# Sums of input blocks taken from PSUM while rows are turned, turns tied behind named products, and four raw weight buffers in a ConvFFN kernel

## The chip, the cores and the metric

The kernel runs on one core of one Trainium2 chip. The metric is the device time of one execution in microseconds (us). The engines are TensorE (PE, matmuls; PEld are its weight loads), VectorE (DVE), ScalarE (ACT), GpSimd (POOL) and SyncE (SP, which here starts the weight transfers). Each engine works its own list in order and waits where an input or a buffer isn't ready.

## The reference

One layer of a decoder for 512 prompt rows, 16 meta rows and 8 × 8 sample rows, D = 1024, D_FF = 2816. The change lies between the token mixing and the end of the ConvFFN:

```python
    mix = jax.nn.sigmoid(gate_a) * (o_a @ p['w_branch_a']) + jax.nn.sigmoid(gate_b) * (o_b @ p['w_branch_b'])
    x = x + rmsnorm(mix @ p['w_out'], p['ln_mix_post'])

    xn = rmsnorm(x, p['ln_ffn_pre'])
    up, gate = jnp.split(xn @ p['w_ffn_in'], 2, axis=-1)
    gate, new_ffn_conv = causal_dwconv(gate, ffn_conv_buf, p['ffn_conv_w'], p['ffn_conv_b'])
    x = x + rmsnorm((jax.nn.gelu(gate) * up) @ p['w_down'], p['ln_ffn_post'])
```

All is float32. The product `mix @ w_out`, the product `xn @ w_ffn_in` and the convolution, Gelu and gating behind it are what the change rearranges.

## The kernel before

**Split products.** A float32 product is made of three matmuls over parts: each operand is divided into `hi` (ACT casts it, line 315) and `lo` (DVE takes the difference, line 316). Line 273 issues every matmul, line 421 every transpose. Tiles `whi`/`wlo` and `hw`/`lw` are weights, `owhi`/`owlo` the two halves of w_out, `fhi11` to `flo22` the turned rows (first digit: half of D, second: half of the columns), `gt` in the output projection the mixed rows.

**Output projection** (`out_proj`). Five row tiles i (0: 64 sample and 2 meta rows; 1 to 4: 128 prompt rows each) times two halves g of w_out: ten products (i, g), each 24 matmuls of 512 columns. After a tile's second product `finish` normalises, adds the residual, normalises again (y), has PE turn the rows (eight transposes to two PSUM banks) and splits them into `fhi`/`flo`. The scheduler places the transposes with a lowered priority.

**ConvFFN input** (`ffn_in`). w_ffn_in has 22 column blocks m of 128 for the gate and 22 for the value u. Blocks m = 0, 1, 2 are plain: four products per block (gate and u, column half 0 and 1) of 24 matmuls. `conv` then runs the gate through line 1804 (ACT), 1806 (two DVE steps) and Gelu (line 1809, ACT), and `times` (1819, 1820) multiplies by u straight from PSUM, which frees u's bank. `differences` makes r1 to r4, sums of blocks of the turned rows, line 1638, on DVE and POOL, and splits them to `fhit`/`flot`.

**The loop**, m = 3 to 21, is a seven-product scheme: p1, p7 of the block before, p5, p2, p6, p4 of the block before, p3, each 12 matmuls. Weights are combined from the four 512-row blocks a11, a12 (gate, tiles `wraw`) and a21, a22 (u, tiles `raw`): POOL makes s1 = a21 + a22 and s3 = a11 − a21, DVE makes s2 = s1 − a11 and s4 = a12 − s2 (tile `sw`, line 1718), and each is divided into `hw`/`lw`. a22 is divided as block "22". Line 1752 is ACT's copy of a product that others are added to, lines 1758 to 1764 add it to the gate (`add_g`), line 1829 adds p7 to u half 1, and then p4 accumulates on the same bank. Three buffers for `raw` and the order of the program decide when SP can start a transfer. Order within an engine is set by the scheduler from the program's order, priorities and buffers.

Of the kernel before, what the change touches and what calls it, by code (L numbers as in the profile page):

```python
# [20 lines left out]
NB = 8  # L21
# [129 lines left out]
class Body:  # L151
# [39 lines left out]
    def run(self):  # L191
# [14 lines left out]
        with ExitStack() as sm:  # L206
# [50 lines left out]
            for key in ("12", "22"):  # L257
                for e in self.f[key]:
                    nc.scalar.copy(e[:, :, 288:290], self.c("zero").unsqueeze(2).to_broadcast([128, 4, 2]))
            with ExitStack() as s:  # L260
                self.out_proj(self.pool(s, "wout"), wo0)
            swo.close()
            self.ftpool = self.pool(sm, "ft", side="right")
            self.ffn_in(sf, self.pool(sm, "gx", side="right"))
# [5 lines left out]
    def mm(self, out, lhsT, rhs, **kw):  # L270
        n = math.prod(rhs.shape[1:])
        self.work += (1.68e-3 if lhsT.dtype == F32 and lhsT.shape[1] > 32 else 0.42e-3) * n
        self.nc.tensor.matmul(out, lhsT, rhs, **kw)  # L273
# [970 lines left out]
    def meta_attention(self, pool):  # L1244
# [5 lines left out]
        mx = self.t(self.small, [128, 1], "mmx")  # L1250
# [36 lines left out]
    def prompt_rows(self, pool, h, st, on, order):  # L1287
# [3 lines left out]
        for i in order:  # L1291
            n = NM + 128 * (i + 1)
            pr = [self.t(pool, [128, 528], f"S{m}", bufs=2) for m in range(2)]
            mxs = [self.t(self.small, [128, 2], "mx", bufs=4) for m in range(2)]
# [14 lines left out]
            for s, mx in zip(pr, mxs):  # L1309
                nm = self.t(self.small, [128, 1], "nm", bufs=4)  # L1310
                nc.vector.tensor_scalar(nm, mx[:, 1:2], -1.0, None, op0=ALU.mult)
                sm = self.t(self.small, [128, 1], "sm", bufs=4)
                nc.scalar.activation(s[:, :n], s[:, :n], AF.Exp, bias=nm, accum_out=sm)
                rc = self.t(self.small, [128, 1], "rc", bufs=4)
# [27 lines left out]
    def head_norm(self, pool, on):  # L1342
        nc = self.nc
        rows, nh = on.shape[0], on.shape[1]
        ss = self.t(self.small, [128, 4], "hss", bufs=2)[:rows, :nh]
# [9 lines left out]
    def sample_attention(self, pool):  # L1355
# [33 lines left out]
        for pr in range(NB // 2):  # L1389
# [3 lines left out]
            mx = self.t(self.small, [128, 5], "smx", bufs=2)  # L1393
# [33 lines left out]
            m1 = self.t(self.small, [128, 1], "m1", bufs=2)  # L1427
# [52 lines left out]
    def soft(self, S, mx, kind):  # L1480
        nc = self.nc
        nm = self.t(self.small, [128, 1], "nm", bufs=4)
        nc.vector.tensor_scalar(nm, mx, -1.0, None, op0=ALU.mult)
        sm = self.t(self.small, [128, 1], "sm", bufs=4)
        nc.scalar.activation(S, S, AF.Exp, bias=nm, accum_out=sm)
        rs = self.t(self.small, [128, 1], "rc", bufs=4)
# [61 lines left out]
    def out_proj(self, pool, wo0):  # L1548
        nc, a = self.nc, self.a
# [8 lines left out]
        ys, sums = {}, {}  # L1558

        def product(i, g):  # L1560
# [3 lines left out]
            for k in range(8):  # L1564
                mh, ml = (e[:, c0 : c0 + n] for e in self.mixed[k])
                self.mm(p[:n], mh, whi[:, k], start=k == 0, stop=False)
                self.mm(p[:n], mh, wlo[:, k], start=False, stop=False)
                self.mm(p[:n], ml, whi[:, k], start=False, stop=k == 7)
            if g == 0:
                ys[i] = self.t(pool, [128, D], "y", bufs=4)  # L1570
# [5 lines left out]
        def finish(i):  # L1576
# [12 lines left out]
            xs = ys.pop(i)  # L1589
# [8 lines left out]
            with self.tc.high_priority(offset=-LATER):  # L1598
                for g in range(2):
# [4 lines left out]
                    if i:  # L1604
                        c = 128 * ((i - 1) % 2)
                        self.put_f(g, i > 2, slice(c, c + 128), p)
                    else:
                        self.put_f(g, 0, slice(288, 290), p[:, :, NS : NS + 2])
                        for half in range(2):
                            self.put_f(g, half, slice(256, 288), p[:, :, 32 * half : 32 * half + 32])  # L1610

        for i, g in ((0, 0), (1, 0), (2, 0), (0, 1), (1, 1), (3, 0), (2, 1), (3, 1), (4, 0), (4, 1)):
            product(i, g)
            if g:
                finish(i)
# [9 lines left out]
    def differences(self, gx, e):  # L1625

        f = self.f
        k = slice(2 * e, 2 * e + 2)
        (h11, l11), (h12, l12), (h21, l21), (h22, l22) = (
            (u[:, k].bitcast(F32) for u in f[key]) for key in ("11", "12", "21", "22")  # L1630
        )
        r1, r2, r3, r4 = (
            self.t(gx, [128, 2 * NC], f"gf{NF - 4 + j}").rearrange("p (k c) -> p k c", k=2) for j in range(4)
        )
        v, g = self.nc.vector, self.nc.gpsimd

        def op(eng, out, a, b, o=ALU.subtract):
            eng.tensor_tensor(out=out, in0=a, in1=b, op=o)

        def part(j, r):  # L1640
            hi, lo = (u[:, k] for u in f[f"t{j}"])
            self.split(hi, lo, r)

        op(v, r1, h12, h11)
        op(g, r3, h22, h12)
        op(v, r1, r1, l11)
        op(v, r1, r1, l12, ALU.add)
        op(g, r3, r3, l22, ALU.add)
        op(v, r2, h22, r1)
        op(v, r2, r2, l22, ALU.add)  # L1650
        op(g, r3, r3, l12)
        part(1, r1)
        part(2, r2)
        op(g, r4, h21, r2)
        op(g, r4, r4, l21, ALU.add)
        part(3, r3)
        part(4, r4)


    def ffn_consts(self, pool):  # L1660

        nc, a = self.nc, self.a
        fw = self.t(pool, [128, NF, 20], "fw", bufs=1)
        rows = []
        for tag, k0, k1 in (("flot4", 0, 9), ("fhit4", 9, 18), ("flot3", 18, NF)):
# [13 lines left out]
        return fw, turn  # L1679

    def ffn_in(self, sf, gx):
# [11 lines left out]
        fw, turn = self.ffn_consts(pool)  # L1693
        for j in range(1, 5):
            f[f"t{j}"] = tuple(self.block_t(p, j) for p in ("hi", "lo"))
# [4 lines left out]
        def weights_g(m):  # L1700
            st = {"m": m, "raw": self.raw_w(w, DFF + 128 * m)}
            hi, lo = self.split_w(st["raw"])
            st["11"], st["12"] = (hi[:4], lo[:4]), (hi[4:], lo[4:])
            return st

        def load_u(st):
            raw = []
            for k in (0, 512):
                t = self.t(w7, [128, 4, 128], "raw", bufs=3)
                nc.sync.dma_start(  # L1710
                    t, w[k : k + 512, 128 * st["m"] : 128 * st["m"] + 128].rearrange("(k p) c -> p k c", p=128)
                )
                raw.append(t)
            st["rawu"] = raw

# [5 lines left out]
        def divide(st, key, src=None):  # L1721
            hi, lo = (self.t(w7, [128, 4, 128], tag, F32R, bufs=n) for tag, n in (("hw", 7), ("lw", 6)))
# [3 lines left out]
        def weights_s(st):  # L1726
# [4 lines left out]
            combine(st, "s4", a12, st["rs2"], ALU.subtract, nc.vector)  # L1731
            divide(st, "s2")
            divide(st, "s4")

        def weights_r(st):
            (a11, a12), (a21, a22) = st["raw"], st["rawu"]
            combine(st, "s3", a11, a21, ALU.subtract)
            divide(st, "s3")
# [10 lines left out]
        def saved(ps, tag):  # L1749
            n = NC if tag == "p1" else NC - 2  # L1750
            t = self.t(pool, [128, n], tag, bufs=2 if tag == "p5" else 1)
            nc.scalar.copy(t, ps[:, :n])
            return t

        def add_g(st, half, ps, t):
            pre = st["pre"]
            sv = pre[:, 514:].rearrange("p (b j) -> p b j", b=NB)
            nc.vector.tensor_tensor(
                out=pre[:, 256 * half + 2 : 256 * half + 258], in0=ps[:, 0:256], in1=t[:, 0:256], op=ALU.add
            )  # L1760
            if half == 0:
                nc.vector.tensor_tensor(out=pre[:, 0:2], in0=ps[:, 288:290], in1=t[:, 288:290], op=ALU.add)
            ss = lambda u: u[:, 256:288].rearrange("p (b t) -> p b t", b=4)
# [50 lines left out]
        def times(eng, st, half, u):  # L1814
            if gfs[st["m"]] is None:
# [3 lines left out]
            eng.tensor_tensor(out=gf[:, sl], in0=y_[:, sl], in1=u[:, 0:256], op=ALU.mult)  # L1819
# [3 lines left out]
                in1=u[:, 256:288].rearrange("p (b t) -> p b t", b=4),  # L1823
# [3 lines left out]
        def p7(st):  # L1827
            product(st["A"], st["s3"], f["t3"], False)
            nc.vector.tensor_tensor(out=st["p5"], in0=st["A"][:, : NC - 2], in1=st["p5"], op=ALU.add)  # L1829
# [23 lines left out]
        def plain(ps, w, half, n):  # L1853

            his, los = w
# [243 lines left out]
```

## Time and profile before

| | |
|---|---|
| median of 3 runs | 1218.4 us (1217.69 to 1219.33) |
| profiled execution | 1217.38 us, span 1215.6 us |
| mean granted clock of TensorE | 0.985 |
| PE, DVE, ACT, POOL busy | 1143.0, 748.4, 502.8, 299.4 us |
| output projection, turns, plain blocks | 710.25 to 827.04 us of the span |
| loop m = 3 to 21 | 827.04 to 1051.11 us |

A row of a timeline is: start in us from the span's start, duration in us, engine, line, operation, output<-inputs, shapes, count, and in brackets the idle time ahead of it and what ended it. SPq and ACTq are the queues that issue transfers. A row of waits is: who <- for whom: total us, times, longest us. A row of windows is: stretch: its length, busy time and instructions of PE, PEld, DVE, ACT and POOL, granted clock, share of the DMA engines, GB/s.

### The profile page before, as it was taken

What the parts mean: (1) busy time and instruction counts of PE and PEld (TensorE: products, weight loads), DVE (VectorE), ACT (ScalarE), POOL (GpSimd) and SP (SyncE); (2) the same over time, 40 slices, a digit from 0 to 9 for tenths busy, and PEclk for the clock granted to TensorE, in tenths of its full rate; (3) what the DMA queues carried; (4) which work ended last, traced back from release to release, by engine and by line L of the source; (5) the groups of instructions that cost most, each with busy time, mean ns of one, the idle gap of its engine ahead of it and who ended that gap; (6) DMA issues with size and microseconds to landing.
All of it is one profiled execution on the core that took longest, in us unless ns stands there. A gap on an engine that the chain in (4) does not pass through costs nothing.

```text
span 1215.6 us, 23653 instructions
## 1 busy us (share of the span) xinstructions
PE 1143.0 (94%) x8683; PEld 1013.7 (83%) x8683; DVE 748.4 (62%) x1888; ACT 502.8 (41%) x1244; POOL 299.4 (25%) x395
## 2 busy tenths in 40 slices
PE   6999999979999988999999999889999999999996
PEld 5887787757677676589998987789999999999996
DVE  5456667596387378346236753698888888942223
ACT  5244445443343243342324433445545454832321
POOL 2122221150241231221010002564444454300000
PEclk9999999999999999999999999989999999999998
DMA  6364525736936846723221452313333332432222
GB/s 197 77 237 133 160 60 179 238 121 192 305 115 192 291 154 201 236 62 87 70 70 54 142 168 92 120 54 97 88 88 88 89 90 86 146 89 72 79 84 82
DMA packets 184059, 157.56 MB, mean 130 GB/s; under 512 B 12538, under 2 KB 146241, under 8 KB 183943
## 3 DMA queue, kind: packets, MB, share of 16 engines
q1 hardware_dynamic: 179569, 147.53, 39.8%
q0 software_dynamic: 3264, 5.16, 1.4%
q10 hardware_dynamic: 1110, 3.35, 0.9%
q8 instruction: 69, 1.13, 0.4%
q14 instruction: 47, 0.39, 0.1%
HBM read 146.12 MB, written 9.88 MB: 128 GB/s over the span
## 4 chain that ended last, share of the span: by engine, by line
PE 52%; DVE 17%; issue 15%; DMA 6%; POOL 5%; ACT 3%; SPq 0%; ACTq 0%; DVEq 0%; POOLq 0%
PE ps_d L273 22%; PE ps_g L273 9%; PE ps_t L273 8%; PE ps_s L273 6%; PE ps_t L421 6%; DMA raw<-in_w_ffn_in 2%; POOL sw L1718 2%; DVE lw L316 2%; DVE cy L651 1%; DMA page<-in_cache_v 1%; PE ps_m L273 1%; DVE KT L1405 1%; DVE fy L1806 1%; DVE gt L316 1%; DVE sw L1718 1%
## 5 line engine op out<-in xcount | busy, mean ns | idle before, releaser
L316 DVE TENSOR_TENSOR wlo<-wraw,whi 128x512 fp32r<-128x512 f32 x196 | 149.7, 779 | 142.4 <-ACT whi L315 140.6
L273 PE MATMUL ps_d<-xhi,whi 128*128 128x256 f32 (+2 forms) x704 | 219.1, 312 | 0.2 <-DVE qm L1135 0.2
L273 PE MATMUL ps_d<-xhi,wlo 128*128 128x256 f32 (+2 forms) x704 | 213.6, 304 | 1.2 <-DVE wlo L316 1.2
L273 PE MATMUL ps_d<-xlo,whi 128*128 128x256 f32 (+2 forms) x704 | 213.3, 303 | 0.3 <-DVE xlo L316 0.2
L315 ACT CAST whi<-wraw 128x512 fp32r<-128x512 f32 x198 | 116.7, 611 | 163.9 <-PE ps_d L273 85.6
L273 PEld LDWEIGHTS ps_d<-xhi,whi 128*128 128x128 f32 x704 | 134.3, 191 | 7.7 <-issue 4.5
L273 PEld LDWEIGHTS ps_d<-xlo,whi 128*128 128x128 f32 x704 | 134.2, 191 | 3.6 <-issue 2.5
L273 PEld LDWEIGHTS ps_d<-xhi,wlo 128*128 128x128 f32 x704 | 133.8, 190 | 2.6 <-DVE wlo L316 1.6
L421 PE MATMUL ps_t<-consts,page 128*128 128x128 f32 x512 | 73.5, 283 | 8.6 <-DVE KT L1405 7.5
L421 PEld LDWEIGHTS ps_t<-consts,page 128*128 128x128 f32 x512 | 57.5, 143 | 25.3 <-issue 10.3
L273 PE MATMUL ps_t<-fhit,hw 128*128 128x290 f32 x228 | 70.7, 310 | 3.7 <-DVE p L1829 3.1
L273 PE MATMUL ps_t<-flot,hw 128*128 128x290 f32 x228 | 67.6, 296 | 0.0
L273 PE MATMUL ps_t<-fhit,lw 128*128 128x290 f32 x228 | 67.5, 296 | 0.0
L1405 ACT COPY KT<-ps_t 128x512 f32<-128x512 f32 x64 | 37.5, 585 | 65.2 <-PE ps_t L421 62.5
L316 DVE TENSOR_TENSOR lw<-sw,hw 128x512 fp32r<-128x512 f32 x76 | 62.4, 821 | 0.3 <-ACT hw L315 0.2
L1405 DVE COPY KT<-ps_t 128x512 f32<-128x512 f32 x64 | 43.7, 685 | 17.7 <-PE ps_t L421 17.5
L273 PEld LDWEIGHTS ps_t<-fhit,hw 128*128 128x128 f32 x228 | 42.9, 188 | 9.4 <-DVE p L1829 6.4
L315 ACT CAST hw<-sw 128x512 fp32r<-128x512 f32 x76 | 46.9, 617 | 7.3 <-POOL sw L1718 5.0
L1804 ACT ACTIVATE fy<-fpre,fw 128x592 f32<-128x592 f32 x22 | 19.4, 884 | 71.5 <-DVE fpre L1764 71.4
L273 PEld LDWEIGHTS ps_t<-flot,hw 128*128 128x128 f32 x228 | 43.3, 190 | 0.0
L273 PEld LDWEIGHTS ps_t<-fhit,lw 128*128 128x128 f32 x228 | 43.1, 189 | 0.0
L273 PE MATMUL ps_s<-KT,qb 128*32 128x256 f32 x512 | 37.8, 401 | 1.3 <-DVE KT L1405 1.1
(665 smaller groups left out, 3122.8 us busy)
## 6 DMA issues: line engine op xcount, KB each, us to landing
page<-in_cache_k SPq DMA_DIRECT2D x128, 256.0 KB, 4.4
page<-in_cache_v SPq DMA_DIRECT2D x128, 256.0 KB, 4.3
wraw<-in_w_in SPq DMA_DIRECT2D x88, 256.0 KB, 3.0
wraw<-in_w_ffn_in SPq DMA_DIRECT2D x50, 256.0 KB, 3.1
wraw<-in_w_down SPq DMA_DIRECT2D x40, 256.0 KB, 3.0
raw<-in_w_ffn_in SPq DMA_DIRECT2D x38, 256.0 KB, 3.0
wraw<-in_w_out SPq DMA_DIRECT2D x16, 256.0 KB
x<-in_x_prompt SPq DMA_DIRECT2D x4, 512.0 KB, 9.0
```

The lines of the kernel that those rows point to most:

```text
L273: self.nc.tensor.matmul(out, lhsT, rhs, **kw)
L315: self.nc.scalar.copy(hi, raw)
L316: (eng or self.nc.vector).tensor_tensor(out=lo, in0=raw, in1=hi.bitcast(F32), op=ALU.subtract)
L421: self.nc.tensor.transpose(out, in_, self.ident[:k, :k])
L651: nc.vector.scalar_tensor_tensor(out=y, in0=pre[:, j : j + n], scalar=self.cw[:, ch, 24 + j : 25 + j], in1=y, op0=ALU.mult, op1=ALU.add)
L1405: (nc.scalar.copy if j % 2 else nc.vector.tensor_copy)(kt[:, :, 128 * j : 128 * j + 128], tp)
L1718: eng.tensor_tensor(out=t, in0=x, in1=y, op=op)
L1804: nc.scalar.activation(y, pre[:, 0:592], AF.Identity, bias=fw[:, m, 19:20], scale=fw[:, m, 16:17])
L1806: nc.vector.scalar_tensor_tensor(out=y, in0=pre[:, j : j + 592], scalar=fw[:, m, 16 + j : 17 + j], in1=y, op0=ALU.mult, op1=ALU.add)
```

## The change

It has five parts. (1) In every turned tile the 34 sample and meta columns stand first, the prompt's behind them, so both halves are 290 wide and one small copy or sum per block falls away. (2) `finish` no longer turns. `turn(i, end)` does, and ties the transposes behind a named matmul: the product order is (0,0), (1,0), (0,1), (1,1), (2,0), turn 0, (3,0), turn 1, (4,0), (2,1), (3,1), (4,1), turn 2, g0, turn 3, u0, the turn of constants, turn 4; g0 and u0 are the first plain products of `ffn_in` (block 0, half 0). (3) A Gelu of one column behind (0,0) brings its table in there. (4) For row tiles 3 and 4 DVE makes r1 and r2 from the transposes' PSUM banks; POOL makes the sample columns of r1 and r2, and all of r3 and r4 (eight operations of 128x580). (5) `raw` has four buffers, `hw` six (before: seven); the loads for block m + 1 are issued behind p1, `raw` ahead of `wraw`; POOL's s3 follows s4 directly and is divided later.

```diff
-        for i, g in ((0, 0), (1, 0), (2, 0), (0, 1), (1, 1), (3, 0), (2, 1), (3, 1), (4, 0), (4, 1)):
-            product(i, g)
-            if g:
-                finish(i)
+        def turn(i, end):
+            n, xs, ps = self.TILES[i][1], ys.pop(i), []
+            with self.tc.issue_after(end):
+                for g in range(2):
+                    p = self.ps4("t")
+                    for k in range(4):
+                        ch = 4 * g + k
+                        self.transpose(p[:, k, :n], xs[:n, 128 * ch : 128 * ch + 128])
+                    ps.append(p)
+            c = 128 * ((i - 1) % 2) + 34
+            c = slice(c, c + 128)
...
+            if i > 2:
+                r1, r2 = (r[:, :, c] for r in self.r12)
+                h11, l11 = (e.bitcast(F32)[:, :, c] for e in f["11"])
+                nc.vector.tensor_tensor(out=r1, in0=ps[0], in1=h11, op=ALU.subtract)
+                nc.vector.tensor_tensor(out=r1, in0=r1, in1=l11, op=ALU.subtract)
+                nc.vector.tensor_tensor(out=r2, in0=ps[1], in1=r1, op=ALU.subtract)
...
+        nc.scalar.activation(warm[:n], sums[0][:n, 0:1], AF.Gelu_apprx_tanh)
+        product(1, 0)
+        product(0, 1)
+        finish(0)
+        product(1, 1)
+        finish(1)
+        product(2, 0)
+        turn(0, ends[2, 0])
+        product(3, 0)
+        turn(1, ends[3, 0])
+        product(4, 0)
...
+        product(4, 1)
+        finish(4)
+        turn(2, ends["half"])
+        g0 = first(DFF)
+        turn(3, g0[2])
+        u0 = first(0)
+        with self.tc.issue_after(u0[2]):
+            turn_consts()
+        turn(4, u0[2])
...
+                if j == 4:
+                    op(r, h21, r2[:, ks])
+                    op(r, r, l21, ALU.add)
+                else:
+                    op(r, r2[:, ks], h11)
+                    op(r, r, l11)
...
-                t = self.t(w7, [128, 4, 128], "raw", bufs=3)
+                t = self.t(w7, [128, 4, 128], "raw", bufs=4)
...
-            hi, lo = (self.t(w7, [128, 4, 128], tag, F32R, bufs=n) for tag, n in (("hw", 7), ("lw", 6)))
+            hi, lo = (self.t(w7, [128, 4, 128], tag, F32R, bufs=n) for tag, n in (("hw", 6), ("lw", 6)))
...
             combine(st, "s4", a12, st["rs2"], ALU.subtract, nc.vector)
+            combine(st, "s3", a11, a21, ALU.subtract)
             divide(st, "s2")
             divide(st, "s4")
...
             p1(st)
+            if m + 1 < NF:
+                nxt = loads(m + 1)
             if last:
                 p7(last)
```

Three places show what the scheduler makes of it. First PE in the output projection, behind (1,0), the last rows of which write ps_d. The row behind it was the first matmul of (2,0), from `owhi` number 1617 (the first half of w_out), and the first of (0,1), from number 1731 (the second half), stood 24 rows later:

```order
L273 MATMUL ps_d_9304<-owhi_1617_8596,gt_9211 128x512
L273 MATMUL ps_g_9333<-owhi_1617_8596,gt_8667 128x512
...
L273 MATMUL ps_g_9333<-owlo_1618_8597,gt_9210 128x512
L273 MATMUL ps_g_9333<-owhi_1617_8596,gt_9211 128x512
L273 MATMUL ps_g_9362<-owhi_1731_9236,gt_8667 66x512
```

Now the first matmuls of (0,1), (1,1) and (2,0) stand there, two of the three from the second half, and then the rest of (0,1):

```order
L271 MATMUL ps_d_9306<-owhi_1617_8596,gt_9211 128x512
L271 MATMUL ps_g_9335<-owhi_1731_9236,gt_8667 66x512
L271 MATMUL ps_g_9382<-owhi_1731_9236,gt_8667 128x512
L271 MATMUL ps_s_9428<-owhi_1617_8596,gt_8667 128x512
L271 MATMUL ps_g_9335<-owlo_1732_9237,gt_8667 66x512
```

The product (0,1) has moved ahead of (2,0). Second, ACT in the plain blocks, about the first block's convolution (fpre to fy). Before, with `gf` the sums that POOL and DVE make:

```order
L1881 COPY fpre_9793<-ps_t_9923 128x256
L1882 COPY fpre_9793<-ps_t_9923 128x4x8
L315 CAST fhit_1825_9778<-gf_1871_10113 128x580
L1804 ACTIVATE fy_9954<-fpre_9793,fw_9761 128x592
L315 CAST whi_10137<-wraw_10135 128x512
L315 CAST fhit_1821_9774<-gf_1869_10111 128x580
L315 CAST whi_10212<-wraw_10208 128x512
```

And in the changed kernel:

```order
L313 CAST fhit_1901_10288<-gf_1857_10030 128x580
L313 CAST fhit_1901_10288<-gf_1858_10033 128x580
L313 CAST fhit_1903_10294<-gf_1859_10036 128x580
L313 CAST fhit_1903_10294<-gf_1860_10039 128x580
L313 CAST whi_10118<-wraw_10114 128x512
L1926 COPY fpre_9880<-ps_d_9965 128x256
L1927 COPY fpre_9880<-ps_d_9965 128x4x8
L313 CAST whi_10118<-wraw_10116 128x512
L1863 ACTIVATE fy_9996<-fpre_9880,fw_9555 128x592
```

All four casts of r4 and r3 have moved ahead of the copies and the convolution of block 0. Third, SP in the loop, where order reads alike and the brackets tell which engine a transfer waits for. Before:

```order
L1710 DMA raw_10987<-in_w_ffn_in 128x4x128 [waits DMAHW3_49,DVE_49,Activation_49]
L1710 DMA raw_10989<-in_w_ffn_in 128x4x128 [waits DMAHW6_49,Pool_49]
L311 DMA wraw_11131<-in_w_ffn_in 128x4x128 [waits DMAHW4_49]
L311 DMA wraw_11133<-in_w_ffn_in 128x4x128 [waits DMAHW1_49,DVE_49,Activation_49]
L1710 DMA raw_11142<-in_w_ffn_in 128x4x128 [waits DMAHW7_49,DVE_49,Activation_49]
```

And in the changed kernel, where raw_10914 and raw_10916 belong to one block and raw_11068 and raw_11070 to the next:

```order
L309 DMA wraw_10920<-in_w_ffn_in 128x4x128 [waits DMAHW6_49,DVE_49,Activation_49]
L1773 DMA raw_10916<-in_w_ffn_in 128x4x128 [waits DMAHW3_49,DVE_49]
L1773 DMA raw_11068<-in_w_ffn_in 128x4x128 [waits DMAHW4_49,Pool_49]
L309 DMA wraw_11072<-in_w_ffn_in 128x4x128 [waits DMAHW5_49]
L309 DMA wraw_11074<-in_w_ffn_in 128x4x128 [waits DMAHW2_49,DVE_49,Activation_49]
L1773 DMA raw_11070<-in_w_ffn_in 128x4x128 [waits DMAHW7_49,DVE_49]
```

The load that waits for POOL was the second of a block and is now the first of the block after; the second now waits for DVE alone.

275 lines of the change are left out of this document (148 added, 127 removed).

## The prediction

> **What bounds the kernel now.** I read the page's engine shares first, then busy time by stage, then the list of waits in the two stages that the change touches, and last single instructions of one loop iteration. TensorE (PE) is busy for 94% of the span, so only its idle time and its half-clock time can be won.
>
> ```profile
> PE 1143.0 (94%) x8683; PEld 1013.7 (83%) x8683; DVE 748.4 (62%) x1888; ACT 502.8 (41%) x1244; POOL 299.4 (25%) x395
> ...
> 869.21:1038.07 168.86, 165.13 (x1183) 159.35 (x1181) 144.72 (x267) 87.23 (x172) 79.27 (x105) 1.00 0.30 87
> 857.94:869.21 11.27, 11.27 (x86) 11.27 (x85) 9.49 (x18) 5.96 (x12) 5.14 (x7) 1.00 0.33 95
> 905.30:917.44 12.14, 11.82 (x87) 11.36 (x86) 10.35 (x20) 6.20 (x13) 5.45 (x8) 1.00 0.31 88
> 710.25:827.04 116.79, 106.18 (x592) 90.14 (x590) 75.51 (x113) 50.74 (x110) 47.05 (x44) 0.96 0.35 109
> ```
>
> The last four rows are stretches of the span: length, then busy time of PE, weight load, DVE, ACT, POOL, then the granted clock. 857.94:869.21 is one iteration of the seven-product loop in which PE never waits: 11.27 us. 869.21:1038.07 holds the next 14 iterations in 168.86 us, 12.06 us each. The loop therefore loses 168.86 − 14 × 11.27 = 11.1 us there. PE's count hides it, since its modelled ends reach over short stops. The waits of those 14 iterations say who is late:
>
> ```profile
> POOL sw L1718 <- DMA raw<-in_w_ffn_in: 35.2, 14, 2.7
> DVE sw L1718 <- POOL sw L1718: 23.2, 14, 1.9
> ...
> PEld ps_t L273 <- DVE p L1829: 6.4, 14, 0.5
> ...
> PEld ps_t L273 <- ACT p L1752: 2.5, 9, 0.5
> ```
>
> Once in each iteration a transfer is late for POOL, POOL is late for DVE, and DVE is late for PE. One iteration in order:
>
> ```profile
> 902.58 2.93 SPq L1710 DMA_DIRECT2D raw<-in_w_ffn_in  x2
> ...
> 903.80 1.31 POOL L1718 TENSOR_TENSOR sw<-wraw,raw 128x512 f32<-128x512 f32 x1
> ...
> 908.29 1.29 POOL L1718 TENSOR_TENSOR sw<-raw,raw 128x512 f32<-128x512 f32 x1 [2.58 <-DMA raw<-in_w_ffn_in]
> ...
> 907.22 0.68 DVE L316 TENSOR_TENSOR lw<-sw,hw 128x512 fp32r<-128x512 f32 x1
> 909.62 0.69 DVE L1718 TENSOR_TENSOR sw<-sw,wraw 128x512 f32<-128x512 f32 x1 [1.72 <-POOL sw L1718]
> ...
> 913.60 0.45 DVE L1829 TENSOR_TENSOR p<-ps_t,p 128x288 f32<-128x288 f32 x1
> ...
> 914.57 1.24 DVE L316 TENSOR_TENSOR lw<-sw,hw 128x512 fp32r<-128x512 f32 x1
> ...
> 914.11 0.40 PE L273 MATMUL ps_t<-fhit,hw 128*128 128x290 f32 x1 [0.22 <-DVE p L1829]
> ```
>
> SP's second transfer waits for a buffer that POOL's s3 (903.80, ends 905.11) still reads. It lands about 3 us later, POOL's s1 runs 908.29 to 909.58, DVE's s2 stands still for 1.72 us, everything behind it on DVE is late, and p4 waits for L1829.
>
> The stage ahead of the loop (710.25:827.04) holds the output projection, the turns and the three plain blocks:
>
> ```profile
> PE ps_s L273 <- ACT fhit L315: 4.6, 1, 4.6
> PE ps_t L421 <- DVE y L405: 3.7, 4, 1.6
> PE ps_t L273 <- ACT hw L315: 2.0, 1, 2.0
> PE ps_t L273 <- DVE lw L316: 0.2, 1, 0.2
> ...
> 786.57:789.99 3.42, 3.42 (x16) 3.42 (x16) 3.42 (x4) 0.92 (x2) 3.26 (x3) 0.50 0.47 137
> 806.99:810.47 3.48, 0.00 (x0) 0.00 (x0) 3.48 (x7) 3.04 (x6) 1.85 (x1) 1.00 0.06 18
> 810.47:817.29 6.82, 5.70 (x24) 5.73 (x25) 6.71 (x11) 2.99 (x6) 4.63 (x5) 0.50 0.27 77
> 817.29:827.04 9.75, 9.75 (x74) 9.75 (x74) 8.05 (x14) 5.94 (x15) 5.49 (x6) 1.00 0.29 82
> ```
>
> PE waits 10.5 us in all, and twice the granted clock falls to 0.50 after a wait. At full clock a matmul of a plain product takes 9.75/74 = 0.132 us, so a product of 24 takes 3.2. At 810.47 one took 5.70, 2.5 more; the window at 786.57 cost half of its 3.42, 1.7.
>
> **The change part by part.** *Raw weights in four buffers, loaded after p1.* SP's second raw load now waits for DVE's lw of block 22 (before: POOL's s3), which stands right behind L1829 and so ends 4 us or more before POOL is free for s1. With 3 us of transfer the data lie there when POOL gets to s1. POOL leaves s3 at 905.11 and does one copy of 0.66, so s1 could run 905.8 to 907.1, ahead of the 907.9 at which DVE becomes free. The 1.72 us wait on DVE goes, and p4 and p6 lose their waits. What is late next: s1 used to run while DVE stood idle and will now run beside DVE's work. The row at 914.57 (1.24 us beside POOL, against 0.68 at 907.22) prices such an overlap at 0.56. DVE then needs 10.35 + 0.56 = 10.9 us, PE 11.27: PE stays the bound, with 0.36 to spare. The sixth instead of seventh hw buffer makes ACT's casts wait for a product's last matmuls, an iteration before their use: hidden by that iteration unless DVE fills up (third rival). Of 11.1 us I take 10.8; bounds 5 (DVE at 11.7) and 11.1.
>
> *New product order, turns behind named products.* The waits for y (3.7), for hw (2.0), for lw (0.2) and the window at 786.57 (1.7) go: −7.6, since two products lie between a row tile's last product and its turn. What is late next is read here:
>
> ```profile
> 721.35 0.39 PE L273 MATMUL ps_g<-owhi,gt 128*128 128x512 f32 x1
> 721.58 0.39 PE L273 MATMUL ps_g<-owlo,gt 128*128 128x512 f32 x1
> ...
> 723.52 0.62 ACT L315 CAST owhi<-wraw 128x512 fp32r<-128x512 f32 x1 [2.04 <-DMA wraw<-in_w_out]
> ...
> 746.62 0.59 ACT L315 CAST fhi<-ps_t 128x512 fp32r<-128x512 f32 x1 [0.78 <-PE ps_t L421]
> ...
> 786.02 0.69 DVE L316 TENSOR_TENSOR flo<-ps_t,fhi 128x512 fp32r<-128x512 f32 x1
> ```
>
> At 721.35 the kernel before begins (2,0), which needs the first half of w_out. The changed one begins (0,1) there, whose first matmul reads all 512 columns of the second half; their last cast for k = 0 waits for a transfer until 723.52 and ends at 724.14. New wait: 724.2 − 721.35 = 2.8 us. Then rows on the clock:
>
> ```profile
> 1182.52:1185.93 3.41, 1.14 (x9) 1.04 (x9) 0.97 (x2) 1.98 (x8) 0.00 (x0) 1.00 0.02 4
> 1185.93:1189.34 3.41, 3.41 (x15) 3.41 (x14) 2.39 (x6) 1.86 (x8) 0.00 (x0) 0.50 0.13 38
> ```
>
> A stretch in which PE worked 1.14 of 3.41 us was followed by 3.41 us at half clock, so I add 1.7 for the new wait. Turns 2 and 4 stand right ahead of products that read their result: a cast (0.59) and a difference (0.69), 1.3 us each. Together +7.1.
>
> *r1 and r2 by DVE from PSUM, r3 and r4 by POOL; Gelu's table early.*
>
> ```profile
> L1638 POOL TENSOR_TENSOR gf<-gf,flo x6: 1751/1790/1843, 787.5 to 812.7; 128x580 f32<-128x580 f32 x6
> ...
> L1638 POOL TENSOR_TENSOR gf<-fhi,gf x2: 1422/1624/1827, 792.5 to 811.2; 128x580 f32<-128x580 f32 x2
> ...
> 804.44 0.68 ACT L315 CAST fhit<-gf 128x580 fp32r<-128x580 f32 x1 [6.66 <-POOL gf L1638]
> 805.02 0.88 ACT L1804 ACTIVATE fy<-fpre,fw 128x592 f32<-128x592 f32 x1
> 805.81 0.61 ACT L315 CAST whi<-wraw 128x512 fp32r<-128x512 f32 x1
> ...
> 808.83 1.28 ACT L1809 ACT_TABLE_LOAD   x1
> 810.12 0.70 ACT L1809 ACTIVATE fy<-fy 128x592 f32<-128x592 f32 x1
> ...
> 811.27 0.17 DVE L1820 TENSOR_TENSOR gt<-fy,ps_s 128x32 f32<-128x32 f32 x1
> ```
>
> The 4.6 us of ps_s ended with the last row, DVE's reading of that bank, though the list names ACT, which came last among its neighbours. The table load leaves the chain that frees ps_s. Early it falls into ACT's wait for owhi and delays a cast that PE doesn't wait for first: 0. But ACT's new order puts the casts of r4 and r3 ahead of whi and of block 0's copy, Gelu and products, and DVE stands behind ACT. From the end of turn 4: cast 0.6, six DVE steps at 0.6 to r2 (4.3 in all), eight POOL operations one after another (11.5 at 1.42 to 15.5 at the 1.9 of POOL beside a full DVE; 13.6 at 1.7, since DVE is emptier), then cast, whi, two copies, whi, fy, two DVE steps, Gelu and products: 5.5. That is 21.3 to 25.3, taken 23.4. PE has six products to do meanwhile, 6 × 3.2 = 19.2, and then waits 4.2 (2.1 to 6.1) where it waited 4.6. The half clock behind it stays: −0.4.
>
> *Rest.* Columns 288 to 290 in half 1 and one small copy or sum less per block: under 0.1 us on PE, nothing on paths. Instructions ahead of the output projection keep their order: 0.
>
> The sum against the profiled run (1217.4 us; its span is 1215.6): −10.8 − 7.6 + 7.1 − 0.4 = −11.7, 1205.7. The median of the three runs is 1.0 above that run, so 1206.7. Its own range is 1204 to 1212, from the loop's bounds and the 4 us of POOL's.
>
> **Rivals.** *First, the half clocks stay away.* If the 2.8 us wait falls over two of the gate's periods, and POOL takes 1.42 each, so that the other wait is 2.1, both slow windows go: −1.7 − 2.5 − 2.1 more, about 1200.4; with only the two windows 1202.5. For it speaks that POOL's early ops took 1.45; against it the row at 1182.52, where 2.27 us without work was enough. The Trainium skill, "TensorE: Matmul & The Clock Gate", section "Part 1: The HAM clock gate", has the half clock only after an idle window of about 3.4 us; by it both windows would go, as here. The trace disagrees with its row of 1.14 busy us. 0.20.
>
> *Second, the loop keeps a wait.* POOL does the products of p7 only after Gelu, then s3, a copy, s1: if s1 still ends after DVE is ready, gain shrinks to between 0 and 5, 1212.5 to 1217.5. For it: POOL's 5.45 us have to fit between Gelu and s2. Against it: the 2.58 us for which POOL itself waits now. 0.17.
>
> *Third, slower.* With six hw buffers four casts per iteration start only when a product ends (0.6 each, as 805.81 shows for a cast of 128x512), and DVE, in order, stands behind each. From DVE's 10.9 us this decides when such waits pass 12.06 − 10.9 = 1.2 per iteration, so when more than two of the four are in DVE's way. With three, 1.8, an iteration takes 12.7 us, 14 of them 9.0 more than before; less the 0.9 that the stage ahead gains, 1226.5. Against it: a DVE that is late finds the casts done. 0.11.
>
> **How the numbers follow.** My forecast has 0.52. 0.2% of 1218.4 is 2.4 us, about what can be told from no change: 1216 to 1220.8. Faster: 0.52 + 0.20 + 0.06 of the second rival's; same: 0.11, the rest of it; slower: 0.11. The range 1199 to 1217 leaves out the third rival and the edges of the others.
>
> **What would show it.** Iterations at 11.3 us from 870 on; no wait of DVE sw for POOL, POOL s1 right behind its copy; a PE wait of 2.8 us at 721.4, two of 1.3 ahead of g0 and of block 0's second gate product; no PE waits for y; a 4 us wait of ps_s at the first product of plain block 2, owned by ACT behind POOL's sums. The prediction is wrong if iterations stay near 12 us or the wait for POOL's sums passes 7 us.

## The result and the profile after

The changed kernel takes 1201.55 us (median of 4 runs, 1199.64 to 1203.08), the kernel before 1218.05 (4 runs, 1215.30 to 1219.33): a ratio of 0.9867 with an interval of 0.9844 to 0.9890. The profiled execution took 1202.23 us, with a span of 1200.2 and a mean granted clock of 0.983. The forecast was 1206.7.

First the engine shares and the stages of the changed kernel, in the columns already used. The second row is the stage ahead of the loop, the third holds 14 iterations of the loop from the fifth on.

```profile
PE 1137.0 (95%) x8683; PEld 1012.3 (84%) x8683; DVE 748.4 (62%) x1863; ACT 508.7 (42%) x1240; POOL 294.0 (24%) x398
...
708.88:824.83 115.95, 107.28 (x593) 90.85 (x590) 69.93 (x109) 50.45 (x105) 45.12 (x47) 0.94 0.37 113
...
866.77:1024.77 158.00, 158.00 (x1182) 157.92 (x1181) 150.51 (x253) 92.20 (x172) 76.78 (x105) 1.00 0.32 93
```

Fourteen iterations take 158.00 us where they took 168.86. The span is 15.4 us shorter, and by PE's matmuls at the borders it divides so:

| part of the span | before | after | difference |
|---|---|---|---|
| ahead of the output projection (same instructions) | 710.26 | 708.88 | −1.38 |
| output projection, turns, plain blocks | 116.78 | 115.95 | −0.83 |
| loop: first 4 iterations | 42.17 | 41.94 | −0.23 |
| loop: next 14 iterations | 168.86 | 158.00 | −10.86 |
| loop: the rest | 17.33 | 15.50 | −1.83 |
| behind the loop | 160.22 | 159.97 | −0.25 |

The waits of the changed kernel from 867 to 1036 us show what became of the loop. No row of POOL for `raw`, none of DVE for POOL and none of PE is left among them. New is that ACT's casts wait for PE and that POOL's s1 waits for DVE, 1.2 us each time:

```profile
ACT hw L313 <- PE ps_t L271: 18.3, 35, 1.0
...
POOL sw L1783 <- DVE lw L314: 15.9, 13, 1.2
...
ACT hw L313 <- PE ps_g L271: 14.4, 14, 1.0
...
DVE lw L314 <- ACT hw L313: 4.3, 14, 0.3
```

One iteration in order. POOL does s3 (907.82), a copy of 0.67, and s1 (910.94); s1 is ready 0.65 us before DVE's s2 (912.88) begins, and s2 doesn't wait. The row at 911.21 shows the price that DVE pays for it: 1.56 us beside s1 instead of 0.68.

```profile
907.82 1.29 POOL L1783 TENSOR_TENSOR sw<-wraw,raw 128x512 f32<-128x512 f32 x1
...
910.94 1.29 POOL L1783 TENSOR_TENSOR sw<-raw,raw 128x512 f32<-128x512 f32 x1 [1.22 <-DVE lw L314]
...
910.18 0.68 DVE L314 TENSOR_TENSOR lw<-sw,hw 128x512 fp32r<-128x512 f32 x1
...
911.21 1.56 DVE L314 TENSOR_TENSOR lw<-sw,hw 128x512 fp32r<-128x512 f32 x1
912.88 0.69 DVE L1783 TENSOR_TENSOR sw<-sw,wraw 128x512 f32<-128x512 f32 x1
```

In the stage ahead of the loop, PE's waits (700 to 830 us), the stretches behind the three longest (724.66, 797.83 and 811.82), and one more at half clock (784.06):

```profile
PE ps_t L271 <- DVE lw L314: 3.2, 1, 3.2
PE ps_g L271 <- ACT owhi L313: 3.2, 1, 3.2
PE ps_s L271 <- DVE gt L1879: 0.8, 1, 0.8
PE ps_t L419 <- DVE y L403: 0.6, 1, 0.6
PE ps_t L419 <- DVE flot L1623: 0.4, 1, 0.4
PE ps_g L271 <- ACT fhi L313: 0.2, 1, 0.2
PE ps_g L271 <- DVE flo L314: 0.2, 1, 0.2
...
724.66:728.08 3.42, 3.42 (x10) 1.87 (x9) 1.49 (x4) 1.27 (x3) 0.00 (x0) 0.50 0.58 170
784.06:787.48 3.42, 2.97 (x15) 2.64 (x13) 2.65 (x6) 2.05 (x6) 1.57 (x3) 0.50 0.76 221
797.83:801.25 3.42, 3.42 (x14) 3.42 (x15) 1.77 (x1) 0.78 (x2) 3.42 (x3) 0.52 0.26 79
811.82:815.30 3.48, 3.48 (x26) 3.48 (x27) 2.79 (x6) 1.98 (x6) 2.44 (x3) 1.00 0.56 151
```

PE waits 8.7 us there (before: 10.6). Half clock follows both waits of 3.2 us and doesn't follow the one of 0.8. The stretch at 784.06 lies at the turns of tiles 3 and 4, where PE waits for no longer than 0.57 us at a time; the kernel before had one of the same length at 786.57, and it had been expected to go. The wait of 3.20 us at 794.63 had not been forecast. DVE, in order, shows its cause:

```profile
790.84 2.61 DVE L314 TENSOR_TENSOR flot<-fhit,fhit 128x1160 fp32r<-128x1160 f32 x1
793.38 2.59 DVE L314 TENSOR_TENSOR flot<-flot,fhit 128x1160 fp32r<-128x1160 f32 x1
795.89 1.89 DVE L314 TENSOR_TENSOR lw<-wraw,hw 128x512 fp32r<-128x512 f32 x1
...
790.56 4.18 POOL L1686 TENSOR_TENSOR gf<-fhi,flot 128x580 f32<-128x580 f32 x2 [3.56 <-DVE flot L1623]
...
802.24 3.36 POOL L1686 TENSOR_TENSOR gf<-gf,flo 128x580 f32<-128x580 f32 x2
```

Two differences of 128x1160 (r1 and r2 divided) stand ahead of the `lw` at 795.89, the second-half weights of plain block 1's u product, for which PE waits until 797.83. All of it runs beside POOL's eight sums, which last from 790.56 to 805.6, 15.0 us, and beside them a DVE step of 0.68 takes 1.9.

### The profile page after: what moved, and what is told of

Read it like the earlier page. It is cut to its first block, busy times and chain, and to the rows that moved or that the text cites. A ratio compares the mean times of both kernels' runs of the same rounds, so it can differ in the third digit from the quotient of the medians.

```text
span 1200.2 us, 23606 instructions
## 1 busy us (share of the span) xinstructions
PE 1137.0 (95%) x8683; PEld 1012.3 (84%) x8683; DVE 748.4 (62%) x1863; ACT 508.7 (42%) x1240; POOL 294.0 (24%) x398
## 4 chain that ended last, share of the span: by engine, by line
PE 67%; DVE 12%; DMA 6%; issue 6%; POOL 4%; ACT 3%; SPq 1%; DVEq 0%; ACTq 0%; POOLq 0%
PE ps_d L271 24%; PE ps_t L271 16%; PE ps_g L271 14%; PE ps_s L271 7%; PE ps_t L419 6%; DMA wraw<-in_w_out 2%; DMA page<-in_cache_v 1%; DVE cy L649 1%; PE ps_m L271 1%; DMA page<-in_cache_k 1%; DVE KT L1403 1%; POOL gf L1686 1%; DVE wlo L314 1%; DMA lk<-in_da_lambda_k 1%; DVE vt L656 1%
## 5 line engine op out<-in xcount | busy, mean ns | idle before, releaser
L419 PEld LDWEIGHTS ps_t<-consts,page 128*128 128x128 f32 x512 | 57.1, 143 | 25.0 <-issue 10.6
L314 DVE TENSOR_TENSOR lw<-sw,hw 128x512 fp32r<-128x512 f32 x76 | 68.7, 905 | 5.3 <-ACT hw L313 5.2
L271 PE MATMUL ps_t<-fhit,hw 128*128 128x290 f32 x228 | 67.5, 296 | 0.0
L1865 DVE SCALAR_TENSOR_TENSOR fy<-fpre,fw,fy 128x592 f32<-128x592 f32 x44 | 36.5, 830 | 0.9 <-ACT fy L1863 0.2
```

What stands on the lines that cost most here:

```text
L271: return self.nc.tensor.matmul(out, lhsT, rhs, **kw).ins
L314: (eng or self.nc.vector).tensor_tensor(out=lo, in0=raw, in1=hi.bitcast(F32), op=ALU.subtract)
L419: self.nc.tensor.transpose(out, in_, self.ident[:k, :k])
L1865: nc.vector.scalar_tensor_tensor(out=y, in0=pre[:, j : j + 592], scalar=fw[:, m, 16 + j : 17 + j], in1=y, op0=ALU.mult, op1=ALU.add)
```

## The experiments

A letter in an expectation stands for the theory that it spells out there. Ratios are to the kernel before on the same chip. "Stage" is the time from the first matmul of the output projection to the loop, in one profiled execution. Two such executions of the same kernel differ by up to 1.5 us there (115.95 and 114.48 for the changed kernel, 113.14 and 111.81 for another version), so a smaller difference of stages says little.

### Which part carries the loop

The kernel before with the buffers of the changed one alone (the place of the loads, the order of s3 and all else as before):

```diff
-                t = self.t(w7, [128, 4, 128], "raw", bufs=3)
+                t = self.t(w7, [128, 4, 128], "raw", bufs=4)
...
-            hi, lo = (self.t(w7, [128, 4, 128], tag, F32R, bufs=n) for tag, n in (("hw", 7), ("lw", 6)))
+            hi, lo = (self.t(w7, [128, 4, 128], tag, F32R, bufs=n) for tag, n in (("hw", 6), ("lw", 6)))
```

> The kernel before with nothing changed but the buffers: raw 4 instead of 3, hw 6 instead of 7; old product order, old sums, old place of the loads and of s3. Theory A (the fourth raw buffer alone carries the loop's gain, since SP's second raw load no longer waits for POOL's s3): the loop's iterations go from 12.06 to 11.3 us, loop -11, the stage ahead unchanged, about 1206 us. Rival B (it takes the earlier loads or the moved s3 as well): iterations stay near 12 us, about 1217 us.

Measured: 1205.68 us, 0.9913 (0.9886 to 0.9939). And the reverse, the changed kernel with three `raw` and seven `hw` buffers:

```diff
-                t = self.t(w7, [128, 4, 128], "raw", bufs=4)
+                t = self.t(w7, [128, 4, 128], "raw", bufs=3)
...
-            hi, lo = (self.t(w7, [128, 4, 128], tag, F32R, bufs=n) for tag, n in (("hw", 6), ("lw", 6)))
+            hi, lo = (self.t(w7, [128, 4, 128], tag, F32R, bufs=n) for tag, n in (("hw", 7), ("lw", 6)))
```

> The changed kernel with raw back at 3 and hw at 7 buffers; all else as changed. Theory A: the loop loses its 11 us again, iterations near 12.0 us, about 1212 to 1214 us. Rival B: iterations stay at 11.3 us and the time at 1201 to 1203 us.

Measured: 1213.70 us, 0.9970 (0.9951 to 0.9990). The 14 iterations from the fifth on, first in the kernel before with four buffers, then in the changed kernel with three, and the waits in the loop of the second:

```profile
871.14:1029.34 158.20, 158.20 (x1183) 158.15 (x1181) 150.34 (x264) 89.31 (x172) 79.42 (x105) 1.00 0.31 90
...
868.93:1036.04 167.11, 164.12 (x1182) 158.90 (x1181) 141.38 (x248) 87.18 (x171) 77.60 (x104) 1.00 0.30 87
...
POOL sw L1783 <- DMA raw<-in_w_ffn_in: 34.1, 13, 2.7
...
DVE sw L1783 <- POOL sw L1783: 23.0, 13, 1.9
```

With the buffers alone the loop runs at PE's pace, 11.3 us an iteration. Without them the earlier loads and the moved s3 win 1.8 us over these 14 iterations, and the late transfer, POOL's wait and DVE's wait of the kernel before stand there again. `hw` was changed in the same step, and no run parts the two; the wait that comes and goes is the one for `raw`, so it is the fourth `raw` buffer that carries the loop. The stage did not share this: in the profile of the first kernel it took 119.21 us, because ACT reached plain block 1's `hw` casts later (a PE wait of 4.4 us instead of 2.0). ACT's queue issued a small transfer of the convolution weights at 784.78 instead of 781.79; what held it up was not followed further.

### The new wait for w_out

In the changed kernel (0,1) needs the second half of w_out at 720.1, before it is there. Here (2,0), which needs the first, goes ahead of it as in the kernel before, and turns 0 to 2 move with it; behind (1,0) stand now:

```diff
+        product(2, 0)
         product(0, 1)
...
-        product(2, 0)
-        turn(0, ends[2, 0])
+        product(2, 1)
+        finish(2)
+        turn(0, ends[2, 1])
         product(3, 0)
         turn(1, ends[3, 0])
         product(4, 0)
+        turn(2, ends[4, 0])
...
-        product(2, 1)
-        finish(2)
...
-        turn(2, ends["half"])
```

> The changed kernel with another product order: (0,0), (1,0), (2,0), (0,1), (1,1), (2,1), turn 0, (3,0), turn 1, (4,0), turn 2, (3,1), (4,1), g0, turn 3, u0, turn of constants, turn 4. Theory C (the wait for the second half of w_out at 720 is plain loss): its 3.2 us, the half-clock stretch behind it (1.7 to 2) and the 0.4 us ahead of g0 go, the plain blocks move forward as a whole: about 1196.5 us. Rival D (the time is given back at turn 0 or at POOL's sums): 1200 to 1202 us.

Measured: 1200.05 us, 0.9868 (0.9841 to 0.9895), against 0.9867 of the changed kernel, stage 114.80. PE's waits in the stage:

```profile
PE ps_t L271 <- DVE lw L314: 3.4, 1, 3.4
PE ps_t L419 <- DVE y L403: 2.7, 1, 2.7
PE ps_t L271 <- DVE y L1575: 1.8, 1, 1.8
PE ps_d L271 <- ACT fhi L313: 0.7, 1, 0.7
```

The wait of 3.2 us is gone, and three others of 5.2 us together have come in where there were 1.4. It is given back, though at turns 3 and 4 and not where the rival put it: turn 2 no longer stands between the last products and the turns of tiles 3 and 4. Counted from the stage's start, PE is ready for turn 4 3.8 us sooner, but DVE's y for tile 4 is ready only 1.7 us sooner, and PE waits for it.

### The wait for lw and the wait for ps_s

The division of r1 and r2 goes behind that of the u weights of plain block 1, on ACT and on DVE:

```diff
-            self.split(hi, lo, r)
+            with self.tc.issue_after(self.mark[0]), self.tc.issue_after(self.mark[1]):
+                self.split(hi, lo, r)
...
-                self.split(hi, lo, raw)
+                self.mark = self.split(hi, lo, raw)
```

> The changed kernel with the split of r1 and r2 queued on ACT and DVE behind the split of plain block 1's value weights, so that PE's 3.2 us wait for lw at 794.6 goes. Theory E (that wait only stands in front of POOL's sums, which free ps_s late whatever PE does): the wait of ps_s at plain block 2 grows from 0.8 to about 4 us, the time stays at 1200 to 1203 us. Rival F (the wait for lw is loss of its own): about 1198.5 us.

Measured: 1200.32 us, 0.9865 (0.9838 to 0.9892), the stage 116.56 in the profile.

```profile
PE ps_s L271 <- ACT fpre L1929: 4.4, 1, 4.4
...
PE ps_t L271 <- DVE lw L314: 0.7, 1, 0.7
```

The wait for `lw` shrinks from 3.2 to 0.7 us, and the one for ps_s grows from 0.8 to 4.4. (The list names ACT there; DVE's last reading of ps_s, which frees the bank, ends 0.15 us before PE goes on.) The two are one bill: PE waits either ahead of the first or ahead of the second. The changed kernel itself, run again further down, divides it a third way, 2.2 and 2.3 us.

So the bill itself has to shrink. On top of that edit, the divisions of r4 and r3 go behind block 0's Gelu (ACT) and its last product with u (DVE):

```diff
-                self.split(hi[:, ks], lo[:, ks], r34.pop(0))
+                with self.tc.issue_after(self.gelu0), self.tc.issue_after(self.times0):
+                    self.split(hi[:, ks], lo[:, ks], r34.pop(0))
```

> The kernel of the run with value weights first, and besides the split of r4 and r3 queued on ACT and DVE behind block 0's Gelu and its products with u, so that ACT doesn't stand behind POOL's sums. Theory E (POOL's sums, through ACT's order, hold ps_s): the 4.4 us wait of ps_s at plain block 2 goes, its place taken by at most 1 us, and the loop begins about 4 us earlier: 1196 us. Rival G (DVE is full between 806 and 826 us, the splits moved there make the loop's first weights late): the time stays at 1199 to 1201 us.

Measured: 1200.27 us, 0.9866 (0.9840 to 0.9893); in the profile the wait for ps_s is 2.2 us and the stage 113.08, 3.5 less than without this edit. Its runs lie between 1197.68 and 1202.03 and their median is that of the run without the edit, so the gain is seen in one profile only, and the 1196 us of the theory did not come. The rival's mechanism isn't seen either: the loop takes 215.5 us in both profiles. With this edit and the order of (2,0) first together:

> The same with the product order (2,0) ahead of (0,1) and turn 2 behind (4,0) as well. Theory C with E: the wait for w_out's second half (3.2 us and a half-clock stretch of about 2) and the two waits at block 2 are gone; what is left are waits for y3 and y4 (1.8 and 2.7 us in the run with that order alone): about 1194 us. Rival: the waits for y take all of it, 1197 to 1200 us.

Measured: 1198.16 us, 0.9843 (0.9817 to 0.9868), stage 113.14. This is the rival's range, and the waits for y are there (2.7 and 1.8 us). And with turn 3 behind u0 besides:

```diff
-        turn(3, g0[2])
...
+            turn(3, u0[2])
```

> The kernel of the run with order and r34, and turn 3 behind u0 instead of g0. Theory J (turn 3's casts on ACT stand ahead of the chain of y4): PE's wait for y ahead of turn 4 (2.7 us) shrinks below 1 us, about 1192.5 us. Rival K (y4 is late by itself, or r1's sums for tile 3 become late): no change against the run with order and r34.

Measured: 1203.27 us, 0.9884 (0.9853 to 0.9914), slower than without it, which neither theory said. PE waits for y not 2.7 but 5.9 us in two places, and the loop's first iteration takes 9.34 us instead of 8.07. The wait, and DVE ahead of its end at 787.15:

```profile
PE ps_t L420 <- DVE y L404: 5.9, 2, 4.5
...
783.69 1.28 DVE L314 TENSOR_TENSOR flo<-ps_t,fhi 128x512 fp32r<-128x512 f32 x2
...
785.50 0.68 DVE L1622 TENSOR_TENSOR fhit<-ps_t,fhi 128x512 f32<-128x512 f32 x1
786.25 0.75 DVE L404 SCALAR_TENSOR_TENSOR y<-xr,r,lnf 128x512 f32<-128x512 f32 x1
```

DVE's reading of turn 3's PSUM (the first two rows) now stands ahead of tile 4's y (the third), and turn 4 waits for that y. So a transpose put off can hold up what stands behind its reading on DVE. That this makes the kernel 5 us slower isn't shown, though: the stage as a whole took 112.84 us, no longer than the 113.14 without this edit, since PE worked 2.4 us less there, with less of it at half clock. Of the 5.4 us between the two profiled executions, 2.3 lie ahead of the stage and 2.2 behind the loop, where nothing was changed, and 1.2 in the loop.

### The early table

The changed kernel without its Gelu of one column, so that the table is loaded where Gelu first runs:

```diff
-        n = self.TILES[0][1]
-        warm = self.t(self.small, [128, 1], "oss1", bufs=2)
-        nc.scalar.activation(warm[:n], sums[0][:n, 0:1], AF.Gelu_apprx_tanh)
```

> The changed kernel without the early Gelu of one column, so that the table is loaded ahead of block 0's Gelu again (1.3 us, on the chain that frees ps_s). Theory H (the load is on that chain only): the wait of ps_s grows from 0.8 to 2.1 us, 1 to 2 us slower than the changed kernel, 1202.5 to 1204 us, with a half-clock stretch behind it at most. Rival I (the chain has room or the early load delays owhi): 1200 to 1202 us and a shorter wait at 720.

Measured: 1205.42 us, 0.9896 (0.9868 to 0.9923), stage 117.84 in the profile. ACT, DVE and PE at the place:

```profile
810.83 1.28 ACT L1865 ACT_TABLE_LOAD   x1
812.24 0.70 ACT L1865 ACTIVATE fy<-fy 128x592 f32<-128x592 f32 x1
...
810.51 1.69 DVE L1862 SCALAR_TENSOR_TENSOR fy<-fpre,fw,fy 128x592 f32<-128x592 f32 x2
...
813.85 0.69 DVE L1780 TENSOR_TENSOR sw<-sw,wraw 128x512 f32<-128x512 f32 x1 [1.05 <-DMA wraw<-in_w_ffn_in]
814.46 0.42 DVE L1875 TENSOR_TENSOR gt<-fy,ps_s 128x256 f32<-128x256 f32 x1
...
815.12 0.37 PE L271 MATMUL ps_s<-fhi,whi 128*128 128x290 f32 x1 [1.02 <-DVE gt L1876]
```

The load itself holds up nothing here. It ends at 812.11, DVE's two steps of the convolution end at 812.20, and Gelu begins at 812.24, right behind DVE as in the changed kernel (810.40 and 810.42): the load fills a wait that ACT has there without it (1.43 us in the changed kernel). What is late is DVE's product. In this kernel's order s2 of the loop's first block stands ahead of it and waits 1.05 us for a transfer, so DVE reads ps_s 1.5 us after Gelu has ended; in the changed kernel it reads at once. Whether the scheduler chose this order because of the load isn't shown. PE's wait for ps_s grew by 0.2 us only, since PE itself came later: behind the wait for `lw` it ran at half clock for 6.83 us instead of 3.41. The Trainium skill, "ScalarE: Activation LUTs", section "What ACT_TABLE_LOAD costs", gives 1283 ns for the load, which the row shows, and about 1.38 us of drain besides, which no gap ahead of 810.83 shows. The stage is 1.9 us longer, about what the additional 3.4 us at half clock cost (half of them, 1.7). The medians differ by 3.9 us, more than this explains, and the intervals of the two ratios overlap; a price of the late load isn't shown.

### POOL beside DVE

The last runs stood side by side on one chip: the changed kernel again, the version with (2,0) first and late r4 and r3 again, and two more built on that version.

> The changed kernel as it is, on the chip of the three runs beside it, for comparison with them: 1200 to 1203 us, iterations of 11.25 us, a wait of 3 us for w_out's second half and together 4 us ahead of block 2.

Measured: 1199.60 us (1198.72 to 1202.01), 0.9866 (0.9846 to 0.9886), stage 114.48. PE waits 3.7 us for w_out's second half, 2.2 for `lw` and 2.3 for ps_s, 4.5 us ahead of block 2 where 4 were expected.

> The kernel of the run with order and r34 again, beside the changed kernel on one chip. Theories C and E: the stage ahead of the loop is 2.8 us shorter (113.1 against 115.95), so the time 2 to 4 us below the changed kernel's. Rival: the difference between the two was the chance of the half-clock stretches: under 1 us.

Measured: 1197.72 us (1196.58 to 1199.32), 0.9848 (0.9831 to 0.9864), stage 111.81. The median is 1.9 us below the changed kernel's beside it, a little less than expected, and the runs of the two overlap.

Then r1 and r2, too, are divided behind block 0's Gelu and products:

```diff
-            with self.tc.issue_after(self.mark[0]), self.tc.issue_after(self.mark[1]):
+            with self.tc.issue_after(self.gelu0), self.tc.issue_after(self.times0):
                 self.split(hi, lo, r)
```

> That kernel with the split of r1 and r2 too behind block 0's Gelu and products with u. Theory L (the last 2.1 us of ps_s's wait are DVE's two differences of 128x1160, 2.0 and 2.6 us, ahead of block 0's convolution): the wait of ps_s goes, stage 111 us, 2 us faster than the run beside it. Rival G (DVE is full up to the loop, the work only moves behind and the loop's p5 waits for r1): the stage shortens and the loop lengthens by as much.

Measured: 1194.42 us (1193.96 to 1198.51), 0.9827 (0.9807 to 0.9847): the best of all, 5.2 us below the changed kernel on this chip, and no run of the one reaches a run of the other. The stage takes 107.83 us. First the two differences and DVE's first reading of block 0's result, as they stood in the version without this edit, then the same with it (also on DVE):

```profile
792.30 1.69 DVE L314 TENSOR_TENSOR flot<-fhit,fhit 128x1160 fp32r<-128x1160 f32 x1 [0.84 <-ACT fhit L313]
793.91 2.60 DVE L314 TENSOR_TENSOR flot<-flot,fhit 128x1160 fp32r<-128x1160 f32 x1
...
805.62 0.42 DVE L1883 TENSOR_TENSOR gt<-fy,ps_s 128x256 f32<-128x256 f32 x1 [0.16 <-ACT fy L1871]
...
803.72 0.41 DVE L1883 TENSOR_TENSOR gt<-fy,ps_s 128x256 f32<-128x256 f32 x1
...
804.57 1.36 DVE L314 TENSOR_TENSOR flot<-fhit,fhit 128x1160 fp32r<-128x1160 f32 x1
805.85 1.36 DVE L314 TENSOR_TENSOR flot<-flot,fhit 128x1160 fp32r<-128x1160 f32 x1
```

Behind POOL's sums the two differences cost 1.36 each; beside them they cost 1.69 and 2.60. DVE frees ps_s earlier and PE does not wait for it. This wait (2.0 us) is half of the 4.0 us that the stage is shorter by; most of the rest is a stretch of 3.41 us at half clock that followed it in the other version (from 806.71) and isn't here. Both theories hold in part: of the stage's 4.0 us the loop's first two iterations take 1.3 back (20.79 us instead of 19.46, with PE waits of 0.6 and 0.2 for ACT's copies of products); what else slows them was not followed.

Last, again on the version with (2,0) first and late r4 and r3, POOL's eight sums themselves go behind block 0's copies on POOL (`tail0` is the last of them):

```diff
+                with self.tc.issue_after(self.tail0):
...
-                    op(r, r2[:, ks], h11)
-                    op(r, r, l11)
+                        op(r, r2[:, ks], h11)
+                        op(r, r, l11)
```

> The kernel of the run with order and r34, with POOL's eight sums queued behind block 0's two tail copies, so that they don't run beside block 0's convolution on DVE. Theory M (a DVE step of 128x512 takes 1.9 us beside POOL's sums and 0.69 without): DVE's steps between 795 and 806 run at 0.7 to 0.8 us, the wait of ps_s goes, and the price moves to block 1 and the loop's first weights; 0 to 2 us either way. Rival N (DVE's steps are slow there for another reason): they stay at 1.9 us.

Measured: 1200.95 us (1199.28 to 1205.50), 0.9877 (0.9849 to 0.9905), slower than that version by 3.2 us, more than the 2 us that the theory allowed. The wait for ps_s is gone here as well, but the price is paid at the loop's start. PE, DVE and POOL:

```profile
820.30 0.40 PE L271 MATMUL ps_t<-fhi,whi 128*128 128x290 f32 x1 [1.30 <-ACT whi L313]
824.10 0.61 PE L271 MATMUL ps_t<-fhi,wlo 128*128 128x290 f32 x1 [3.27 <-DVE wlo L314]
...
802.48 1.93 DVE L314 TENSOR_TENSOR wlo<-wraw,whi 128x512 fp32r<-128x512 f32 x1
804.34 0.41 DVE L1886 TENSOR_TENSOR gt<-fy,ps_s 128x256 f32<-128x256 f32 x1
...
801.89 3.82 POOL L1687 TENSOR_TENSOR gf<-gf,flo 128x580 f32<-128x580 f32 x2
```

The sums now run from 798.1 to 812.7, beside the division of the weights for block 2 and for the loop, and slow those from 0.68 to 1.93 us. DVE comes late to the loop, PE waits 4.6 us for its weights, and the first iteration takes 13.89 us. Putting the sums off moves the overlap to work that PE needs sooner; putting DVE's work off (the run ahead) takes it out of the overlap.

## Why the prediction was right or wrong

- **The loop, forecast −10.8 us.** Measured −10.86 in the same 14 iterations. Mechanism and cause hold: the late transfer, POOL's wait and DVE's wait are gone with the fourth buffer and return without it. DVE's load was put at 10.9 us per iteration; it is 150.51/14 = 10.75. One detail differs: s1 doesn't follow its copy at once but waits 1.22 us for DVE's `lw` ahead of it (907.82 to 910.94 above), and still is in time. One margin was smaller than read: DVE's `lw` of block 22 ended at 906.69, 3.0 us and not 4 or more before POOL was done with the copy (909.72). A load takes 2.9 to 3.0 us to land, so it came just in time, with s1's wait for `lw` behind it as the margin.
- **Third rival, six `hw` buffers.** Its mechanism came, its price did not. The casts wait for PE 49 times in 15 iterations, more than three of four casts each time, past the number from which it was to decide (in the kernel before with the buffers alone they wait for PE too). But DVE stood behind a cast only once an iteration, for 0.3 us: the casts that wait are ahead of DVE's need. The step that failed there is that each late cast stops DVE.
- **The stage, forecast −0.9 (−7.6, +7.1, −0.4).** Measured −0.83: right as a sum, and by luck, since terms that were off offset one another. PE waited 1.9 us less than before and was busy for 1.1 us more, with 13.7 us of the stage at half clock instead of 10.2. The wait for w_out's second half was 3.19 us (2.8 forecast), and the half clock behind it lasted twice as long as reckoned (6.83 us from 722.62). The waits that were to go shrank as said, but y kept 0.6, with 0.4 for `flot` beside it, and the half-clock window that was to go with them (1.7) came again, at 784.06. Of the two waits of 1.3 us for turned rows, the one ahead of g0 was 0.4 and the other none that the list shows; why they shrank was not followed. The wait for ps_s was 0.83 instead of 4.2.
- **The mis-sized term: POOL's sums.** They took 15.0 us, near the upper bound of 15.5, not 13.6, since DVE beside them was not as empty as the prediction took it. And the price of the overlap on DVE was counted in the loop only. In the stage it made two differences of 128x1160 take 2.6 us each, and PE waited 3.20 us for the `lw` behind them. This wait stands ahead of ps_s's and took most of that one's place; the run with r1 and r2 divided later shows that they are one bill. The half clock expected at ps_s came at that wait instead (0.52 from 797.83).
- **The table, forecast 0.** No run shows another price. In the kernel before the load did stand on the chain that frees ps_s (DVE's steps ended at 808.47, Gelu began at 810.12, right behind the load); put back into the changed kernel, it fills a wait of ACT.
- **First rival, the half clocks stay away.** The time, 1201.55, lies in the 1200.4 to 1202.5 that it gave, but not by its mechanism: three stretches at half clock came.
- **Second rival.** No iteration keeps a wait of PE, or of DVE for POOL.
- **The 5 us below the forecast.** 1.4 us lie ahead of the output projection, where nothing was changed: the time to its first matmul runs from 706.8 to 711.9 us over the kernels here. PE was no less busy there than before (667.7 against 666.9 us), so it waited less; why was not followed. The forecast also added 1.0 us for the median over the profiled execution, and the median then lay 0.7 below it. The loop's end gave 1.83 that had not been counted. Half of that is a wait of PE in the kernel before, just ahead of the last products (from 1038 to 1056):

```profile
PE ps_s L421 <- POOL ftail L1801: 0.9, 1, 0.9
```

## What to carry to other kernels

When a chain of late transfer, helper engine and main engine repeats in each iteration, price the one buffer that starts it: here it brought 11 us of 15, and all that was moved around it a few. When a wait is taken away, list what the waiting engine has next and whether that is ready; two waits in a row on one chain are one bill, and only work that is shorter or stands off that chain pays it. Where two engines slow each other, move the work of the one that PE waits for out of the overlap, and look at what the overlap then falls on.

## What the runs showed of the hardware

POOL's sums slow DVE, and DVE's steps slow POOL: beside each other 128x512 from SBUF takes DVE up to 1.9 us instead of 0.68, 128x1160 takes 2.6 instead of 1.36, and a sum of 128x580 takes POOL 1.9 (3.82 for two) where the quickest in the kernel before took 1.42. How the two share isn't shown. A DVE step that reads one operand from PSUM isn't touched: 0.41 us at 804.34 in the midst of a POOL sum, as 0.41 without one at 803.72 in the version ahead. The Trainium skill, "SBUF — State Buffer", section "Who interferes with whom", says that a DVE instruction with two SBUF inputs contends with a GpSimd instruction that reads SBUF, and that one with at most one SBUF input, outside the two-port modes, does not. These rows agree.

Half clock followed waits of 3.19 and 3.20 us, and one of 2.04 in the second version of the last runs (granted clock 0.50 from 806.71). It did not follow one of 0.83, nor waits of 2.16 and 2.32 us in the changed kernel run again (1.00), so the length of a wait alone doesn't decide it. With it, time wanders in parts that no edit touched: the stretch behind the loop took 159.90 us at a granted clock of 0.97 in the changed kernel, and 158.20 at 0.98 in the second version of the last runs. Differences of 2 us between single executions therefore need several runs.
